# Weight tiles of the FFN: two buffers for weight sums and six for plain blocks become one ring of eight fixed tiles

## Chip, cores and metric

The kernel runs on one core of one Trainium2 chip. The metric is the device time of one execution in microseconds (us). A measurement of this kernel can tell about 0.2%, some 4.2 us, from no change.

## What is computed

The reference is a decoder trunk of two layers over a residual stream of 256 tokens by 2048 columns, all float32:

```python
for layer in range(DEPTH):                       # DEPTH = 2
    xn = rms_norm(h, norm_mix[layer])
    mix = swa_mlstm_mixer(xn, ...) if layer % 2 == 0 else forgetting_attention_mixer(xn, ...)
    h = h + mix                                  # both end in ... @ w_out
    h = h + swiglu(rms_norm(h, norm_ffn[layer]), w_gate[layer], w_up[layer], w_down[layer])
return rms_norm(h, norm_final)

def swiglu(xn, w_gate, w_up, w_down):            # 2048 -> 5632 -> 2048
    return (jax.nn.silu(xn @ w_gate) * (xn @ w_up)) @ w_down
```

Layer 0 mixes with sliding-window attention and an mLSTM side by side, layer 1 with a forgetting attention of 16 heads. Each mixer ends in an output projection (2048 by 2048), and the FFN follows.

## The kernel before, in words

**Split products.** [...] A weight block arrives by DMA as `raw` (128 x 1024, two k-tiles of 512 columns); ScalarE copies it to `hi` (line 180), VectorE forms `lo = raw - hi` (line 181), and TensorE adds three products per k-tile and half of the tokens: hi by hi, lo by hi, hi by lo (`three`, line 524, and lines 215 to 217 in `gemm`). So each weight byte costs a cast on ScalarE and a subtraction on VectorE before TensorE may read it.

**Chunks and blocks.** `gemm` (line 196) runs a projection as a row of such chunks. The FFN and some other products run in `pair_group` (line 532): two matrices side by side, walked in blocks of two k-tiles. A plain block (kind 0) takes one chunk of each matrix: two `hi`/`lo` pairs, 24 matmuls. A mixed block (kind 1) replaces products of the two token halves and the two matrices by sums, in the manner of Strassen: 21 matmuls instead of 24, but VectorE forms four sums of weights (lines 601 to 604), and four pairs are split: the first matrix's chunk (`hg`, `lg`), half a chunk of the second (`hu`, `lu`, line 600), and two pairs of sums, called the halves (`hs`, `ls`, line 613; their tiles are `ht` and `lt`).

**Buffers.** `hi` and `lo` come from the pool `wp`, six buffers each (line 103). The halves come from the FFN's own pool `fp`, two buffers each of `ht` and `lt` (lines 611 and 612), that is, just one mixed block's worth. Outside the FFN, mixed blocks use other spare memory for their halves (`spare_halves`, line 494). `raw` has four buffers in `wr` for plain chunks and four in `fp` for mixed blocks. The pool `fp` opens in `close_layer` (line 759), which runs the output projection (`out_proj`, line 503) and then the FFN (`ffn`, line 632); its memory is what the mixers' pools have given back.

**Order.** The FFN is cut into parts of 3, 4 and 4 column groups (`PARTS`), each followed by its share of the down projection. A group walks eight blocks in `ORDER` (five plain, three mixed) or, for the groups in `DENSE` (1, 4, 6, 8), in `HEAVY` (four and four); `DOWN` does the same for the down projection. Transposes of the activations run by DMA and are joined some blocks later (`join`, line 695). The Tile framework orders each engine's instructions when the kernel is built, and every engine then works through its own fixed order, waiting on semaphores. The loads of weights are all issued by SyncE, in the order in which the program names them. The output projection's chunks are ordered among the last steps of the mixer (the mLSTM heads, `mlstm`, line 1073, in layer 0; the last quarter of the attention, `attention`, line 372, in layer 1): its products over the first twelve k-tiles need nothing of those steps.

Of the kernel before, what the change touches and what calls it, by code (L numbers as in the profile page):

```python
# [9 lines left out]
F32R = mybir.dt.float32r  # L10
# [7 lines left out]
P = 128  # L18
# [5 lines left out]
NB = 512  # L24
CK = 2
# [50 lines left out]
def trunk(  # L76
# [23 lines left out]
    xl = sp_.tile([P, KT, S], F32R, name="xl")  # L100
    mh = sp_.tile([P, KT, S], F32R, name="mh")
    ml = sp_.tile([P, KT, S], F32R, name="ml")
    wp = ctx.enter_context(tc.tile_pool(name="wp", bufs=6))
    wr = ctx.enter_context(tc.tile_pool(name="wr", bufs=4))
    cp = ctx.enter_context(tc.tile_pool(name="cp", bufs=1))
    sm = ctx.enter_context(tc.tile_pool(name="sm", bufs=2))
# [65 lines left out]
    def load_chunk(w, k0, c0, n):  # L172
        raw = ahead.pop(0) if ahead else load_raw(w, k0, c0, n)
        return raw if isinstance(raw, tuple) else split_chunk(raw, n)

    def split_chunk(raw, n):
        hi = wp.tile([P, CK, NB], F32R, tag="hi", name="hi")
        lo = wp.tile([P, CK, NB], F32R, tag="lo", name="lo")
        for k in (slice(0, 1), slice(1, CK)) if any(raw is f for f in fine) else (slice(0, CK),):
            latest[0] = nc.scalar.copy(hi[:, k, 0:n], raw[:, k, 0:n])  # L180
            nc.vector.tensor_tensor(  # L181
                out=lo[:, k, 0:n], in0=raw[:, k, 0:n], in1=hi[:, k, 0:n].bitcast(F32), op=ALU.subtract
            )
        return hi, lo
# [6 lines left out]
    def run_due(todo, step):  # L191
        while todo and todo[0][0] <= step:
            with tc.issue_after(latest[0].ins):
                todo.pop(0)[1]()
# [334 lines left out]
    def bank(par, name):  # L529
        return pm.tile([P, NB], F32, tag="pm", name=name) if par else pa.tile([P, NB], F32, tag="acc", name=name)  # L530

    def pair_group(fp, par, lhs, sums, mats, order, todo=(), halves=None, inner=None, raws=None):
        plain = [[bank(par, "acc") for _ in range(NT)] for _ in range(2)]
        begun = set()

        def fresh(*at):
            known = at in begun
            begun.add(at)
            return not known

        todo = list(todo)
        prods = None
        kinds = [kind for kind, _ in order]
        t0, t1 = slice(0, P), slice(P, 2 * P)

        def combine(prods):
            c = fp.tile([P, 4, NB], F32, tag="c", name="c", bufs=1)
            nc.scalar.copy(c[:, 0, :], prods[0])
            if halves is None:
                nc.vector.tensor_tensor(out=c[:, 1, :], in0=prods[3], in1=c[:, 0, :], op=ALU.add)  # L550
                nc.vector.tensor_tensor(out=c[:, 2, :], in0=prods[2], in1=c[:, 1, :], op=ALU.add)  # L551
                nc.vector.tensor_tensor(
                    out=c[:, 1:4:2, :],
                    in0=prods[1].rearrange("p (a n) -> p a n", a=1).broadcast_to([P, 2, NB]),
                    in1=c[:, 1:3, :],
                    op=ALU.add,
                )
                return c
            nc.vector.tensor_tensor(out=c[:, 2, :], in0=prods[3], in1=c[:, 0, :], op=ALU.add)
            nc.vector.tensor_tensor(out=c[:, 1, :], in0=prods[2], in1=c[:, 2, :], op=ALU.add)  # L560
            nc.vector.tensor_tensor(out=c[:, 3, :], in0=prods[1], in1=c[:, 1, :], op=ALU.add)
            nc.vector.tensor_tensor(out=c[:, 2, :], in0=prods[1], in1=c[:, 2, :], op=ALU.add)
            return c

        for pos, (kind, pair) in enumerate(order):
            k0 = 2 * pair
            if inner is not None and pos == len(order) - 1:
                c = combine(prods)
                inner()
            if not kind:  # L570
                last = pos == len(order) - 1
                walk = [(i, t) for i in range(CK) for t in range(NT)]
                if last:
                    walk.sort(key=lambda it: it[1])
                for m, (w, c0) in enumerate(mats):
                    hi, lo = load_chunk(w, k0, c0, NB)
                    run_due(todo, pos)
                    for i, t in walk:
                        ah, al = lhs(k0 + i)
                        ts = slice(t * P, (t + 1) * P)  # L580
                        three(
                            plain[m][t], ah[:, ts], al[:, ts], hi[:, i, :], lo[:, i, :],
                            fresh(m, t), last and i == CK - 1,
                        )
                continue
            first, last = 1 not in kinds[:pos], 1 not in kinds[pos + 1 :]
            if first:
                prods = [bank(1 - par, "prod") for _ in range(4)]
            ra, rb = (load_raw(w, k0, c0, NB, fp, W_RAWS if halves else RAWS, raws) for w, c0 in mats)
            hg, lg = split_chunk(ra, NB)  # L590
            run_due(todo, pos)
            t4 = ra if halves else fp.tile([P, 2, NB], F32, tag="t4", name="t4", bufs=1)
            ta, tb, tc_, td = (
                (ra[:, 0, :], rb[:, 0, :], rb[:, 1, :], ra[:, 1, :])
                if halves
                else (t4[:, 0, :], t4[:, 1, :], ra[:, 0, :], ra[:, 1, :])
            )
            hu = wp.tile([P, CK, NB], F32R, tag="hi", name="hi")
            lu = wp.tile([P, CK, NB], F32R, tag="lo", name="lo")
            split_plain(hu[:, 1, :], lu[:, 1, :], rb[:, 1, :])  # L600
            nc.vector.tensor_tensor(out=ta, in0=rb[:, 0, :], in1=ra[:, 0, :], op=ALU.subtract)
            nc.vector.tensor_tensor(out=tb, in0=rb[:, 1, :], in1=rb[:, 0, :], op=ALU.subtract)
            nc.vector.tensor_tensor(out=tc_, in0=rb[:, 1, :], in1=ta, op=ALU.subtract)
            nc.vector.tensor_tensor(out=td, in0=ra[:, 1, :], in1=tc_, op=ALU.subtract)
            parts = []
            for src in (ra, rb) if halves else (t4, ra):
                if halves:
                    hs, ls = halves.pop(0)
                    halves.append((hs, ls))
                else:  # L610
                    hs = fp.tile([P, 2, NB], F32R, tag="ht", name="ht")
                    ls = fp.tile([P, 2, NB], F32R, tag="lt", name="lt")
                split_plain(hs, ls, src)
                parts.append((hs, ls))
            where = ((0, 0), (1, 0), (1, 1), (0, 1)) if halves else ((0, 0), (0, 1), (1, 0), (1, 1))
            ht = [parts[a][0][:, b, :] for a, b in where]
            lt = [parts[a][1][:, b, :] for a, b in where]
            sh, sl = sums(pair)
            xa, la = lhs(k0)
            xb, lb = lhs(k0 + 1)  # L620
            three(prods[0], xa[:, t0], la[:, t0], hg[:, 0, :], lg[:, 0, :], first, last)
            three(plain[0][0], xb[:, t0], lb[:, t0], hg[:, 1, :], lg[:, 1, :], fresh(0, 0), False)
            three(plain[1][0], sh[3], sl[3], hu[:, 1, :], lu[:, 1, :], fresh(1, 0), False)
            three(prods[1], sh[0], sl[0], ht[0], lt[0], first, last)
            three(prods[2], sh[2], sl[2], ht[1], lt[1], first, last)
            three(prods[3], sh[1], sl[1], ht[2], lt[2], first, last)
            three(plain[0][1], xb[:, t1], lb[:, t1], ht[3], lt[3], fresh(0, 1), False)
        if inner is None:
            c = combine(prods)
        return plain, c  # L630
# [128 lines left out]
    def close_layer(layer, w_out, idx, key, **rest):  # L759
        with tc.tile_pool(name=f"fp{layer}", bufs=2) as fp:  # L760
            nx = len(mixed_of(ORDER))
            nd = max(len(mixed_of(o)) for o in DOWN.values())
            sx = [fp.tile([P, nx, 4, P], F32R, name=f"sx{i}", bufs=1) for i in range(2)]
            x4 = fp.tile([P, 2, P], F32R, name="x4", bufs=1)
            todo = out_proj(w_out, idx, key, (*sx, x4, fp))
            sd = [fp.tile([P, nd, 4, P], F32R, tag=f"sd{i}", name=f"sd{i}", bufs=1) for i in range(2)]
            ffn(layer, fp, sx, x4, sd, key, todo, **rest)


    acc0 = new_acc()  # L770
    hi = wp.tile([P, CK, NB], F32R, tag="hi", name="hi")
    lo = wp.tile([P, CK, NB], F32R, tag="lo", name="lo")
    latest[0] = latest_warm
    for k in range(CK):
        with tc.issue_after(latest[0].ins):
# [594 lines left out]
```

## Time and profile before

| | |
|---|---|
| median of 3 runs | 2111.59 us (2111.06 to 2115.66) |
| the profiled execution | 2111.82 us |
| its span in the profile | 2110.1 us |
| mean granted TensorE clock | 0.997 |
| VectorE busy | 1854.7 us, 88% |
| ScalarE busy | 1387.9 us, 66% |
| moved by DMA | 434.87 MB, 206 GB/s on average |

Engines: PE is TensorE's matmuls, PEld its weight loads, DVE VectorE, ACT ScalarE, POOL GpSimd, SP SyncE. A group's row gives line, engine, operation and tiles, the count, busy time, mean time of one in ns, and the idle time before them with what ended it. A row of the timeline gives start and duration in us; the bracket is the idle time before it and what ended it. A row of stretches gives each engine's busy time in that stretch and, in brackets with an x, how many instructions it began. Matmuls overlap in the pipeline, so the pace of PE is read from one start to the next.

### The profile page before, as it was taken

The numbers are of one execution on the slowest core, as the hardware profiler recorded it, in microseconds if no ns is written. First come the engines' busy times: TensorE is split into PE (matmuls) and PEld (weight loads), VectorE is DVE, ScalarE is ACT, GpSimd is POOL, SyncE is SP. The second block draws the span as 40 slices with busy tenths as digits, with TensorE's granted clock in tenths as the row PEclk, the third lists the DMA queues.
The fourth block names the chain that finished last, engine by engine and source line by source line (L and its number), as shares of the span: only waits on it lengthen the run. The fifth ranks groups of instructions, "written<-read, shape, count | busy, mean of one in ns | idle before, by whom it ended". The sixth has DMA issues, their size and how long they took to land.

```text
span 2110.1 us, 26965 instructions
## 1 busy us (share of the span) xinstructions
PE 2073.6 (98%) x9449; PEld 1710.7 (81%) x9449; DVE 1854.7 (88%) x2415; ACT 1387.9 (66%) x1760; POOL 43.2 (2%) x66
## 2 busy tenths in 40 slices
PE   9999999999999999999999999999999999999998
PEld 7878888778887788888888888888778887788887
DVE  6788769999998999999899678689999999999995
ACT  6767678665576656666667676687655666556763
POOL 1010100000000000000000001000000000000000
PEclk9999999999999999999999999999999999999999
DMA  8666677666666666766667766596656666756664
GB/s 289 176 201 200 202 238 215 198 209 196 190 217 204 216 195 206 229 201 202 199 196 215 221 201 184 155 276 202 223 188 204 209 203 187 236 191 211 217 189 153
DMA packets 309575, 434.87 MB, mean 206 GB/s; under 512 B 106412, under 2 KB 114624, under 8 KB 309312
## 3 DMA queue, kind: packets, MB, share of 16 engines
q1 hardware_dynamic: 307088, 426.27, 65.4%
q0 software_dynamic: 1632, 5.80, 0.9%
q8 instruction: 74, 1.21, 0.2%
q10 hardware_dynamic: 720, 1.09, 0.1%
q14 instruction: 61, 0.50, 0.1%
HBM read 408.68 MB, written 2.12 MB: 195 GB/s over the span
## 4 chain that ended last, share of the span: by engine, by line
PE 85%; DVE 7%; DMA 3%; issue 2%; ACT 2%; SPq 0%; POOLq 0%; POOL 0%; DVEq 0%; ACTq 0%
PE acc L525 18%; PE acc L526 17%; PE acc L527 17%; PE acc L216 5%; PE acc L215 5%; PE acc L217 5%; PE prod L525 5%; PE prod L527 4%; PE prod L526 4%; DVE lo L181 2%; DMA raw<-in_w_down_dram 2%; DVE lt L350 1%; DMA raw<-in_w_up_dram 1%; PE p L379 1%; PE po L480 1%
## 5 line engine op out<-in xcount | busy, mean ns | idle before, releaser
L180 ACT CAST hi<-raw 128x1024 fp32r<-128x1024 f32 (+3 forms) x648 | 655.2, 1027 | 372.4 <-PE acc L527 216.3
L181 DVE TENSOR_TENSOR lo<-raw,hi 128x1024 fp32r<-128x1024 f32 (+3 forms) x648 | 761.8, 1190 | 115.7 <-ACT hi L180 112.5
L526 PE MATMUL acc<-lo,xh 128*128 128x512 f32 x1198 | 467.2, 390 | 0.0
L527 PE MATMUL acc<-hi,xl 128*128 128x512 f32 x1198 | 463.8, 390 | 0.0
L525 PE MATMUL acc<-hi,xh 128*128 128x512 f32 x1198 | 461.2, 391 | 0.1
L525 PEld LDWEIGHTS acc<-hi,xh 128*128 128x128 f32 x1198 | 225.1, 188 | 48.3 <-DVE c L551 0.8
L526 PEld LDWEIGHTS acc<-lo,xh 128*128 128x128 f32 x1198 | 225.2, 188 | 47.3 <-DVE lo L181 0.8
L527 PEld LDWEIGHTS acc<-hi,xl 128*128 128x128 f32 x1198 | 225.2, 188 | 47.0
L349 ACT CAST ht<-t 128x1024 fp32r<-128x1024 f32 x103 | 108.4, 1052 | 113.6 <-PE prod L527 80.5
L525 PE MATMUL acc<-hi,mh 128*128 128x512 f32 x437 | 167.0, 393 | 10.0 <-ACT mh L349 5.0
L526 PE MATMUL acc<-lo,mh 128*128 128x512 f32 x437 | 170.4, 390 | 0.0
L527 PE MATMUL acc<-hi,ml 128*128 128x512 f32 x437 | 166.1, 389 | 0.0
L350 DVE TENSOR_TENSOR lt<-t,ht 128x1024 fp32r<-128x1024 f32 x103 | 125.6, 1219 | 23.5 <-ACT ht L349 22.7
L350 DVE TENSOR_TENSOR lt<-raw,ht 128x1024 fp32r<-128x1024 f32 x103 | 125.3, 1217 | 3.2 <-ACT ht L349 3.0
L216 PE MATMUL acc<-lo,mh 128*128 128x512 f32 (+1 forms) x322 | 126.3, 392 | 0.0
L215 PE MATMUL acc<-hi,mh 128*128 128x512 f32 (+1 forms) x322 | 125.8, 391 | 0.0
L217 PE MATMUL acc<-hi,ml 128*128 128x512 f32 (+1 forms) x322 | 123.7, 391 | 0.0
L349 ACT CAST hi<-raw 128x512 fp32r<-128x512 f32 x117 | 72.4, 619 | 71.4 <-PE acc L527 49.9
L349 ACT CAST ht<-raw 128x1024 fp32r<-128x1024 f32 x103 | 108.0, 1049 | 13.7 <-PE acc L527 10.2
L525 PEld LDWEIGHTS acc<-hi,mh 128*128 128x128 f32 x437 | 82.0, 188 | 31.6 <-ACT mh L349 6.4
L216 PE MATMUL acc<-lo,xh 128*128 128x512 f32 (+3 forms) x288 | 100.1, 348 | 0.2 <-DVE lo L181 0.2
L217 PE MATMUL acc<-hi,xl 128*128 128x512 f32 (+3 forms) x288 | 99.4, 346 | 0.0
(382 smaller groups left out, 3575.8 us busy)
## 6 DMA issues: line engine op xcount, KB each, us to landing
raw<-in_w_gate_dram SPq DMA_DIRECT2D x176, 512.0 KB, 4.4
raw<-in_w_up_dram SPq DMA_DIRECT2D x176, 512.0 KB, 4.5
raw<-in_w_down_dram SPq DMA_DIRECT2D x176, 512.0 KB, 4.8
raw<-in_w_in_odd_dram SPq DMA_DIRECT2D x88, 512.0 KB, 4.9
raw<-in_w_in_even_dram SPq DMA_DIRECT2D x51, 512.0 KB, 5.0
raw<-in_w_out_even_dram SPq DMA_DIRECT2D x32, 512.0 KB, 5.1
raw<-in_w_out_odd_dram SPq DMA_DIRECT2D x32, 512.0 KB, 4.8
hr<-in_w_in_even_dram SPq DMA_DIRECT2D x12, 512.0 KB, 4.5
```

The source lines that it names most:

```text
L180: latest[0] = nc.scalar.copy(hi[:, k, 0:n], raw[:, k, 0:n])
L181: nc.vector.tensor_tensor(out=lo[:, k, 0:n], in0=raw[:, k, 0:n], in1=hi[:, k, 0:n].bitcast(F32), op=ALU.subtract)
L215: nc.tensor.matmul(o, ah[:, ts], hi, start=(k == 0), stop=False)
L216: nc.tensor.matmul(o, ah[:, ts], lo, start=False, stop=False)
L217: nc.tensor.matmul(o, al[:, ts], hi, start=False, stop=(k == k_all - 1 and cs.stop == n))
L349: nc.scalar.copy(dst_h, src)
L350: nc.vector.tensor_tensor(out=dst_l, in0=src, in1=dst_h.bitcast(F32), op=ALU.subtract)
L379: nc.tensor.matmul(pq[j % 2][:, j // 2, :], q_of(j, b), k_of(j)[:, 0:cols], start=True, stop=True)
L480: nc.tensor.matmul(po, v_of(j, 0), tt[:, j, 0:2, :].rearrange("p c q -> p (c q)"), start=True, stop=False)
L525: nc.tensor.matmul(o, ah, hi, start=start, stop=False)
L526: nc.tensor.matmul(o, ah, lo, start=False, stop=False)
L527: nc.tensor.matmul(o, al, hi, start=False, stop=stop)
```

## The change

The pool `wp` keeps six pairs of tiles, now with fixed names, in a list; `slot()` takes the oldest pair and puts it at the list's end. `close_layer` makes two further pairs in `fp`, in the place of the two buffers each of `ht` and `lt`, and appends them to the list before the output projection; at the end of the layer they leave it. Everything that is split in the FFN, plain chunks and halves alike, and also the chunks of the output projection, takes its pair from this ring of eight. The bytes in use are the same: two buffers each of `ht` and `lt` before, two pairs `hi6`, `lo6`, `hi7`, `lo7` after.

```diff
-    wp = ctx.enter_context(tc.tile_pool(name="wp", bufs=6))
+    wp = ctx.enter_context(tc.tile_pool(name="wp", bufs=1))
+    weights = [[wp.tile([P, CK, NB], F32R, name=f"{a}{i}") for a in ("hi", "lo")] for i in range(6)]
+
+    def slot():
+        weights.append(weights.pop(0))
+        return weights[-1]
...
     def split_chunk(raw, n):
-        hi = wp.tile([P, CK, NB], F32R, tag="hi", name="hi")
-        lo = wp.tile([P, CK, NB], F32R, tag="lo", name="lo")
+        hi, lo = slot()
...
-            hu = wp.tile([P, CK, NB], F32R, tag="hi", name="hi")
-            lu = wp.tile([P, CK, NB], F32R, tag="lo", name="lo")
+            hu, lu = slot()
...
                 else:
-                    hs = fp.tile([P, 2, NB], F32R, tag="ht", name="ht")
-                    ls = fp.tile([P, 2, NB], F32R, tag="lt", name="lt")
+                    hs, ls = slot()
                 split_plain(hs, ls, src)
...
             x4 = fp.tile([P, 2, P], F32R, name="x4", bufs=1)
+            more = [[fp.tile([P, CK, NB], F32R, name=f"{a}{i}", bufs=1) for a in ("hi", "lo")] for i in (6, 7)]
+            weights.extend(more)
             todo = out_proj(w_out, idx, key, (*sx, x4, fp))
             sd = [fp.tile([P, nd, 4, P], F32R, tag=f"sd{i}", name=f"sd{i}", bufs=1) for i in range(2)]
             ffn(layer, fp, sx, x4, sd, key, todo, **rest)
+            for pair in more:
+                weights.remove(pair)
```

The very first chunk of the kernel takes its pair by `slot()` too.

More of the change, by code (lines that the diff above doesn't have):

```diff
@@ L767, in close_layer @@
             ffn(layer, fp, sx, x4, sd, key, todo, **rest)
+            for pair in more:
+                weights.remove(pair)
     acc0 = new_acc()
-    hi = wp.tile([P, CK, NB], F32R, tag="hi", name="hi")
-    lo = wp.tile([P, CK, NB], F32R, tag="lo", name="lo")
+    hi, lo = slot()
     latest[0] = latest_warm
```

## The prediction, made before the changed kernel was run

> **What bounds the kernel now.** I read the page's busy times first:
>
> ```profile
> span 2110.1 us, 26965 instructions
> PE 2073.6 (98%) x9449; PEld 1710.7 (81%) x9449; DVE 1854.7 (88%) x2415; ACT 1387.9 (66%) x1760; POOL 43.2 (2%) x66
> ```
>
> PE has 36.5 us of idle time in all; only what returns some of it, or lets matmuls run closer together, can help. So next I cut the span into stretches of 50 us and looked for those in which PE is not full. A full one stands first, then the eight in the two FFNs that are not:
>
> ```profile
> core 0: us, PE busy (x) PEld busy (x) DVE busy (x) ACT busy (x) POOL busy (x), PEclk, DMA share, GB/s
> 500.00:550.00 50.00, 50.00 (x223) 41.40 (x222) 47.30 (x54) 27.72 (x31) 0.00 (x0) 1.00 0.66 211
> 400.00:450.00 50.00, 47.11 (x198) 37.68 (x197) 45.68 (x58) 31.47 (x35) 0.00 (x0) 0.97 0.66 205
> 450.00:500.00 50.00, 47.16 (x208) 37.88 (x207) 47.91 (x59) 26.14 (x30) 0.00 (x0) 1.00 0.59 187
> 650.00:700.00 50.00, 45.61 (x193) 35.32 (x192) 44.57 (x56) 30.79 (x35) 0.00 (x0) 1.00 0.61 190
> 700.00:750.00 50.00, 48.21 (x210) 38.99 (x209) 48.29 (x56) 31.58 (x33) 0.00 (x0) 1.00 0.67 204
> 1450.00:1500.00 50.00, 48.23 (x210) 38.79 (x209) 46.26 (x59) 32.64 (x37) 0.00 (x0) 1.00 0.65 200
> 1500.00:1550.00 50.00, 47.87 (x212) 38.48 (x211) 48.32 (x60) 33.38 (x38) 0.00 (x0) 1.00 0.68 216
> 1700.00:1750.00 50.00, 48.92 (x214) 39.61 (x212) 42.97 (x57) 33.91 (x37) 0.00 (x0) 1.00 0.68 200
> 1750.00:1800.00 50.00, 44.84 (x188) 34.61 (x189) 49.22 (x59) 34.14 (x38) 0.00 (x0) 1.00 0.67 209
> ```
>
> Two readings. PE is idle for 22.1 us in these eight (50 less each PE busy time, added). But they begin 1633 matmuls where eight full stretches would begin 8 x 222 = 1776: 143 are missing, and at 50 / 222 = 0.225 us each that is **32 us lost**, 10 more than the idle time. VectorE is at 86 to 98% in the same rows, so it has hardly any reserve when it falls behind. The timeline of PE at the first stop shows where the other 10 us are:
>
> ```profile
> 401.06 0.61 PE L525 MATMUL prod<-ht,xh 128*128 128x512 f32 x2
> 404.13 0.50 PE L525 MATMUL prod<-ht,xh 128*128 128x512 f32 x1 [2.45 <-ACT ht L349]
> ...
> 406.66 0.63 PE L526 MATMUL acc<-lo,xh 128*128 128x512 f32 x1
> 407.08 0.63 PE L527 MATMUL acc<-hi,xl 128*128 128x512 f32 x1
> ...
> 408.61 0.40 PE L525 MATMUL acc<-hi,xh 128*128 128x512 f32 x1
> ```
>
> After a stop of 2.45 us the matmuls start 0.42 us apart instead of 0.225 for a while. From 401.06 to 408.61 PE begins 14 matmuls; at full pace they take 3.2 us, here 7.55: the stop with its tail costs 4.4 us, 1.9 more than its length. PE waited for a half (`ht`). What PE waits for in all, and what holds the halves up, is told by the lists of waits of PE and ScalarE, and by VectorE's timeline in the costliest stretch:
>
> ```profile
> PE prod L526 <- DVE lt L350: 5.1, 5, 1.6
> PE prod L525 <- ACT ht L349: 4.4, 4, 2.5
> PE pt L282 <- DVE h L363: 3.7, 1, 3.7
> ACT ht L349 <- PE prod L527: 80.5, 48, 4.1
> 670.24 1.23 DVE L350 TENSOR_TENSOR lt<-t,ht 128x1024 fp32r<-128x1024 f32 x1 [3.27 <-ACT ht L349]
> ```
>
> The halves stand at the head of PE's waits (5.1 and 4.4 us). 48 times a cast into `ht` waits until PE has read the half before it, and at 670 VectorE stands idle for 3.27 us behind such a cast, in a stretch where it is the engine that is late.
>
> **Part 1, the FFN: what the ring gives.** No instruction is added or removed; the built program has the same count on every engine. What moves is which matmul frees the buffer of a cast, and with it the order. In the built orders I counted the matmuls between the last reader of a buffer and the first reader of its next content: for a half the median rises from 28 to about 50, for a plain chunk it falls slightly, from 46 to 44; the tightest twentieth is 16 to 18 in both. So halves gain 5 us of room (22 x 0.225) and plain chunks give up 0.5. The half that was cast just before 670 is freed, in the new assignment, by a matmul that runs at 648 in the trace of before: 20 us earlier.
>
> What that is worth I add up along the queues. A stop arises where, from the matmul that frees a buffer, the queued work of ScalarE and VectorE up to a later operand of PE lasts longer than PE's own matmuls in between. The prices:
>
> ```profile
> L180 ACT CAST hi<-raw 128x1024 fp32r<-128x1024 f32 (+3 forms) x648 | 655.2, 1027 | 372.4 <-PE acc L527 216.3
> L350 DVE TENSOR_TENSOR lt<-t,ht 128x1024 fp32r<-128x1024 f32 x103 | 125.6, 1219 | 23.5 <-ACT ht L349 22.7
> 664.36 0.68 DVE L601 TENSOR_TENSOR t<-raw 128x512 f32<-128x512 f32 x1
> 664.96 0.68 DVE L602 TENSOR_TENSOR t<-raw 128x512 f32<-128x512 f32 x1
> raw<-in_w_down_dram SPq DMA_DIRECT2D x176, 512.0 KB, 4.8
> ```
>
> In a full queue a large VectorE operation takes 1.14 us (a little under its 1.22, since they overlap) and a small one 0.60 (664.96 - 664.36). From the cast before 670 to the matmul that needs the transposed activations (`mh`) stand that cast and a copy (2.8 us), 19 large and 24 small VectorE operations and four tiny ones (37.2 us), one load that they hold back (4.7 us), and three casts and two copies behind it (5.7 us): 50.4 us, against 193 matmuls, 43.8 us. PE comes 6.6 us short. The same walk gives 6.1 us for the stops from 400 to 460, and 6.2 and 6.6 us for their twins in layer 1: 25.6 us in all, between the 22.1 us of idle time and the 32 us with the slow matmuls, which is how far I trust it. Along the built order of the changed kernel, at the same prices, 0.6, 1.4 and 1.4 us remain in layer 0 and 1.4 and 1.4 in layer 1: 6.3 us. Three quarters go: **32 x 19.3 / 25.6 = 24 us gained**. The bounds: no gain, if VectorE is late anyway; 32 us, if every stop goes. The next thing that is late is VectorE itself, in the dense groups.
>
> **Part 2, the output projections: what the ring costs.** The two further pairs join the ring before the output projection, and they lie in `fp`, over memory that the mixer still uses: in layer 0 over the output gates and mLSTM matrices, in layer 1 over the queries, keys and transposed probabilities of the last quarter. Chunks 7 and 8 of each output projection fall to these pairs, and cannot be cast before the mixer has ended. This is an added wait. Behind it stand: the two `raw` tiles that hold these chunks, half of the four that plain loads have; and on PE the chunks' matmuls, which the built order puts behind the mixer's last steps. In before those matmuls are the cover of these steps:
>
> ```profile
> 257.30 0.87 DVE L1097 SCALAR_TENSOR_TENSOR hv<-hv,st,og 128x256 f32<-128x256 f32 x2
> 261.14 0.27 PE L1124 MATMUL ptv<-ident,hv 128*128 128x128 f32 x1
> 1334.15 1.92 DVE L426 TENSOR_SCALAR s<-s,rec 128x128 f32<-128x128 f32 x8
> 1338.86 0.27 PE L466 MATMUL pp<-ident,s 128*128 128x128 f32 x1
> ```
>
> In layer 1 the scaled probabilities are ready at 1336.1 and PE takes them at 1338.9: 2.8 us of reserve. In the changed order 57 matmuls (12.9 us) that stood between the scores and this transpose stand behind it, none ahead. 12.9 - 2.8 = 10.1 us are uncovered; the copy after the transposes, so far behind 15 further matmuls that also move, adds about 0.4, and late loads (below) some. I take 11.5. In layer 0 the head's result is ready at 258.2 and taken at 261.1, a reserve of 3.0 us; 56 matmuls (12.7 us) move behind. That would uncover 9.7 us, but here part of the moved matmuls stood ahead of the mLSTM's own matmuls too, so the chain starts earlier; its queues added up give 6.7. I take 7. The bounds: 5.4 us at each place if only the two chunks' own 24 matmuls count, less the reserve, so 5 in all; and 25.6 if no reserve helps. Each stop is followed by slow matmuls, 1.9 us by the row at 404: 3.8. **Loss 11.5 + 7 + 3.8 = 22 us.**
>
> [...]
>
> **Part 3, the rest.** The two pairs that hold `ht` and `lt` are replaced byte for byte, the six old pairs turn as before, and the mixers' own blocks keep their halves elsewhere. Their order shifts a little, and PE is full there, as the stretches around the two output projections show:
>
> ```profile
> 250.00:300.00 50.00, 50.00 (x226) 41.30 (x226) 30.47 (x49) 35.48 (x59) 1.38 (x2) 1.00 0.65 197
> 1300.00:1350.00 50.00, 50.00 (x249) 42.32 (x248) 33.92 (x49) 27.46 (x42) 1.03 (x1) 1.00 0.62 190
> ```
>
> I price the shift at nothing, from -2 to +2 us. The stop between the layers, 3.7 us before `pt` in the list of waits above, does not hang on weight buffers and stays.
>
> **The sum.** 2111.8 (the profiled execution) - 24 + 22 = **2110 us**, 0.1% below it and below the median of 2111.59, which lies 0.2 us under that execution.
>
> **Rivals.**
> *The stops at the output projections are cheap.* If the scheduler's shift lets the attention and mLSTM chains run as much earlier as PE is freed, only the two chunks' own matmuls lack, less the reserves: 2 x 5.4 - 2.8 - 3.0 = 5 us, with slow tails about 9. Then 2111.8 - 24 + 9 = 2097 us. For it: VectorE does fewer subtractions between scores and probabilities in the new order. Against it: the scores themselves don't come earlier in layer 1.
> *The locked loads decide (slower).* With two of four `raw` tiles held, the next six chunks load in pairs, each pair after the one before it:
>
> ```profile
> raw<-in_w_out_even_dram SPq DMA_DIRECT2D x32, 512.0 KB, 5.1
> raw<-in_w_out_odd_dram SPq DMA_DIRECT2D x32, 512.0 KB, 4.8
> ```
>
> A round is 4.8 to 5.1 + 1.03 + 1.22 = 7.1 to 7.3 us for 24 matmuls, 5.4 us. If PE has nothing else, three rounds cost 3 x 1.7 = 5 us in each layer, 10 in all: 2120 us. It decides from the point at which PE has used what was cast before chunk 7; in the trace those chunks run beside other matmuls, which speaks for less.
> *Short stops do not slow PE.* If the slow matmuls belong to something other than the stops, the FFN can give back only idle time, 22.1 x 3/4 = 17 us, while the two long stops still have their tails: 2111.8 - 17 + 22 = 2117 us. [...]
>
> **How the numbers follow.** The forecast, gain and loss nearly cancelling (2104 to 2116): 0.40. Cheap stops, 2097: 0.26. Locked loads, 2120: 0.26. Short stops free, 2117: 0.08. Of the forecast's 0.40 I put 0.10 on faster by over 0.2% (below 2107.4), 0.24 within 0.2%, which is about what a measurement can tell, and 0.06 slower (above 2115.8). So faster 0.36, same 0.24, slower 0.40. The range takes in the centres of both sides, 2096 to 2122: the bounds of parts 1 and 2 reach further (2085 to 2137), but only with every term at its end.
>
> **What would show it.** Right: in the FFNs' stretches PE begins 215 to 222 matmuls everywhere and the waits for `ht` and `lt` shrink from 9.5 us to under 4. Near 250 and 1320 PE has stops of 6 to 12 us, ended by the mixer's last steps (`ptv`, `pp`), with ScalarE's casts of chunks 7 and 8 after them. Loads of the output projection land in pairs 7 us apart. Wrong: PE full at 250 and 1320 (part 2 falls), or FFN stretches still at 190 to 210 (part 1 falls, VectorE being the bound).

## The result, and the profile after

The changed kernel takes 2116.76 us (median of 10 runs, 2115.35 to 2118.14) against 2111.97 us of the kernel before: a ratio of 1.0021, 95% interval [1.0011, 1.0031]. (One of the ten runs of the kernel before took 2599.66 us; the ratio leaves it out.) It is 4.8 us slower where 2 us faster was forecast; that is just about what a measurement can tell. The profiled execution took 2116.89 us, with this span and PE row:

```profile
span 2115.2 us, 26817 instructions
PE 2074.0 (98%) x9449; PEld 1714.0 (81%) x9449; DVE 1851.3 (88%) x2415; ACT 1382.6 (65%) x1760; POOL 40.8 (2%) x66
```

The totals say nothing: PE's busy time differs by 0.4 us, and each engine has as many instructions as before (the total, 26817 for 26965, counts waiting and issuing instructions too). The stretches of 50 us do. These are the FFNs' eight, with the same columns as in the prediction; the matmuls that ran in a stretch, the one or two under way at its start included, stand behind PE's busy time:

```profile
400.00:450.00 50.00, 48.14 (x212) 39.22 (x211) 48.83 (x64) 35.75 (x41) 0.00 (x0) 1.00 0.70 227
450.00:500.00 50.00, 49.41 (x219) 39.83 (x218) 47.93 (x58) 27.65 (x32) 0.00 (x0) 1.00 0.64 215
650.00:700.00 50.00, 48.23 (x212) 39.14 (x211) 49.21 (x62) 33.10 (x37) 0.00 (x0) 1.00 0.68 216
700.00:750.00 50.00, 50.00 (x223) 41.39 (x222) 47.67 (x57) 30.90 (x34) 0.00 (x0) 1.00 0.62 202
1450.00:1500.00 50.00, 47.89 (x204) 39.14 (x203) 47.24 (x61) 33.34 (x37) 0.00 (x0) 0.97 0.67 205
1500.00:1550.00 50.00, 50.00 (x221) 41.20 (x220) 49.64 (x63) 32.68 (x37) 0.00 (x0) 1.00 0.63 211
1700.00:1750.00 50.00, 49.46 (x218) 40.63 (x217) 46.99 (x60) 35.76 (x39) 0.00 (x0) 1.00 0.59 180
1750.00:1800.00 50.00, 48.75 (x215) 39.92 (x214) 50.00 (x62) 35.92 (x39) 0.00 (x0) 1.00 0.67 214
```

Against 222 matmuls in a full stretch, 22 are missing in layer 0 (the first four rows) and 30 in layer 1. Before, it was 79 and 64. So 57 came back in layer 0 and 34 in layer 1: 91 x 0.225 = 20.5 us. The stretches around the two output projections, full before, went the other way:

```profile
250.00:300.00 50.00, 45.18 (x191) 36.61 (x192) 27.32 (x38) 32.20 (x50) 1.38 (x2) 0.91 0.59 161
1300.00:1350.00 50.00, 39.08 (x190) 32.41 (x189) 30.20 (x46) 24.96 (x41) 0.63 (x1) 0.90 0.46 137
```

They hold 191 matmuls instead of 226 and 190 instead of 249. The list of PE's waits names the stops (total us, times, longest us):

```profile
PE pp L471 <- DVE s L431: 10.5, 1, 10.5
PE acc L220 <- ACT mh L359: 6.9, 1, 6.9
PE acc L530 <- ACT c L553: 3.8, 2, 2.1
PE prod L530 <- DVE xl L360: 3.1, 1, 3.1
PE acc L531 <- DVE lo L186: 2.9, 4, 1.2
...
PE prod L530 <- ACT hi L354: 1.1, 2, 0.5
```

The waits for `ht` and `lt` that led the list before are gone (the halves are now called `hi` and `lo`). At the head stand two stops that the kernel before did not have: 10.5 us before the transposes of the probabilities (layer 1) and 6.9 us before the output projection's own matmuls, which need `mh`, the mixer's activations (layer 0). The stop of 3.7 us before `pt`, which the prediction left in its place, is gone; the one of 3.1 us behind `xl` (the low part of the activations, formed on VectorE) is new.

For a ledger I compared the start of a PE instruction in two traces wherever both programs have sent PE the same instructions up to it (within a few that changed places at the ends of a layer). The difference of two such points says what the stretch between them cost or gave, in us against the trace of before:

| stretch of the span before | forecast | changed | changed, 2nd trace | E1 | E1, 2nd trace | E3 |
|---|---|---|---|---|---|---|
| 184 to 276: output projection, layer 0 | +8.9 | +12.4 | +12.9 | +2.3 | +1.9 | +1.8 |
| 300 to 735: FFN, layer 0 | -12 | -12.3 | -12.5 | -10.6 | -11.2 | -5.1 |
| 735 to 1303: rest of layer 0, mixer of layer 1 | 0 | +1.0 | +1.4 | +2.5 | +2.1 | +4.8 |
| 1303 to 1354: output projection, layer 1 | +13.4 | +12.7 | +12.9 | +0.2 | +0.1 | +0.2 |
| 1369 to 1810: FFN, layer 1 | -12 | -8.0 | -9.4 | -8.8 | -7.7 | 0.0 |

E1 and E3 are experiments below. In the changed kernel the two projections lose 25.1 us and the FFNs give back 20.3.

### The profile page after: what moved, and what is told of

Its sections match the earlier page's. It is cut to its first block, busy times and chain, and to the rows that moved or that the text cites. A ratio compares the mean times of both kernels' runs of the same rounds, so it can differ in the third digit from the quotient of the medians.

```text
span 2115.2 us, 26817 instructions
## 1 busy us (share of the span) xinstructions
PE 2074.0 (98%) x9449; PEld 1714.0 (81%) x9449; DVE 1851.3 (88%) x2415; ACT 1382.6 (65%) x1760; POOL 40.8 (2%) x66
## 4 chain that ended last, share of the span: by engine, by line
PE 82%; DVE 7%; DMA 4%; ACT 3%; issue 3%; SPq 0%; ACTq 0%; POOLq 0%; POOL 0%; DVEq 0%
PE acc L531 18%; PE acc L532 17%; PE acc L530 17%; PE acc L221 5%; PE acc L220 5%; PE acc L222 5%; PE prod L530 4%; PE prod L532 4%; PE prod L531 4%; DVE lo L186 3%; DVE lo L355 2%; ACT hi L185 1%; DMA raw<-in_w_up_dram 1%; DMA raw<-in_w_down_dram 1%; DMA raw<-in_w_in_odd_dram 1%
## 5 line engine op out<-in xcount | busy, mean ns | idle before, releaser
L531 PE MATMUL acc<-lo,xh 128*128 128x512 f32 x1272 | 495.4, 390 | 0.2 <-DVE lo L186 0.2
L532 PE MATMUL acc<-hi,xl 128*128 128x512 f32 x1272 | 493.4, 390 | 0.0
L530 PE MATMUL acc<-hi,xh 128*128 128x512 f32 x1272 | 479.4, 391 | 3.8 <-ACT c L553 3.8
L532 PEld LDWEIGHTS acc<-hi,xl 128*128 128x128 f32 x1272 | 239.3, 188 | 49.8
L354 ACT CAST hi<-raw 128x512 fp32r<-128x512 f32 (+1 forms) x220 | 179.3, 819 | 72.2 <-PE acc L532 44.6
L355 DVE TENSOR_TENSOR lo<-raw,hi 128x512 fp32r<-128x512 f32 (+1 forms) x220 | 204.8, 933 | 11.9 <-ACT hi L354 11.9
L354 ACT CAST hi<-t 128x1024 fp32r<-128x1024 f32 x103 | 108.3, 1051 | 85.3 <-PE prod L532 65.5
L355 DVE TENSOR_TENSOR lo<-t,hi 128x1024 fp32r<-128x1024 f32 x103 | 125.4, 1217 | 11.0 <-ACT hi L354 10.7
L531 PEld LDWEIGHTS acc<-lo,mh 128*128 128x128 f32 x466 | 87.5, 188 | 21.9 <-DVE lo L186 3.9
L532 PEld LDWEIGHTS acc<-hi,ml 128*128 128x128 f32 x466 | 87.5, 188 | 18.1
```

Of the source, the lines that this page charges most:

```text
L354: nc.scalar.copy(dst_h, src)
L355: nc.vector.tensor_tensor(out=dst_l, in0=src, in1=dst_h.bitcast(F32), op=ALU.subtract)
L530: nc.tensor.matmul(o, ah, hi, start=start, stop=False)
L531: nc.tensor.matmul(o, ah, lo, start=False, stop=False)
L532: nc.tensor.matmul(o, al, hi, start=False, stop=stop)
```

## The experiments

The theory after the result: loss and gain are two things with different causes. The loss comes from one chunk in the output projection that cannot be cast before the mixer has ended, and from everything on PE that stands behind it; the gain comes from the later reuse of the halves' buffers, and the stops that remain in the FFN are VectorE's own lateness. The rivals are named with each run.

### Loss and gain taken apart: E1, E2 and E3

E1 lets the two pairs join the ring only behind the output projection:

```
             more = [[fp.tile([P, CK, NB], F32R, name=f"{a}{i}", bufs=1) for a in ("hi", "lo")] for i in (6, 7)]
-            weights.extend(more)
             todo = out_proj(w_out, idx, key, (*sx, x4, fp))
+            weights.extend(more)
```

> The two further pairs join the ring only after the output projection, so that its 32 chunks turn over the six old pairs and the FFN alone over eight. Theory (the two effects are separate: the output projections lose 12.4 and 13.5 us because chunks 7 and 8 fall to pairs over the mixer's memory; the FFNs gain 12.2 and 8.3 us through the ring of eight): the stops of 6.9 and 10.5 us before acc and pp are gone, the FFNs' gain stays, and the time is 2112.0 - 12.2 - 8.3 = 2091.5 us (2087 to 2094). Rival 1 (the stops come from the fixed tiles or from the shifted order of the whole program, not from where the pairs lie): the stops stay, 2110 to 2117 us. Rival 2 (the FFN's gain is only ScalarE and VectorE catching up after a late output projection): without the late start the gain goes too, 2106 to 2112 us.

E2 gives the ring of eight to the output projections alone:

```
             todo = out_proj(w_out, idx, key, (*sx, x4, fp))
+            for pair in more:
+                weights.remove(pair)
+            own[:] = more
...
-                    hs, ls = slot()
+                    own.append(own.pop(0))
+                    hs, ls = own[-1]
```

> The ring of eight serves the output projections alone; for the FFN the two further pairs leave it and hold the halves of the weight sums, as ht and lt did before. Theory (losses and gains are separate and add): 2112.0 + 12.4 + 13.5 = 2137.9 us (2134 to 2141), with the stops before acc (layer 0) and pp (layer 1) at 6 to 11 us. Rival (a late output projection is made up in the FFN whatever its buffers are): 2118 to 2128 us.

E3 has the fixed tiles and shares nothing: `weights.extend(more)` is replaced by `own[:] = more`, ahead of the output projection, and the halves turn over `own` as in E2.

> Only the form is changed: the six pairs are fixed tiles that turn by hand, and the halves turn over two fixed pairs of their own; nothing is shared. Theory: the buffers free as in the kernel before, 2112 us, within 2 us. Rival (fixed tiles make the scheduler order the work in another way and carry part of the loss): 2115 us or more.

| kernel | ring of eight in the projection | in the FFN | median us | ratio to before, 95% interval |
|---|---|---|---|---|
| E3 | no | no | 2114.03 | 1.0002 [0.9993, 1.0012] |
| E2 | yes | no | 2138.71 | 1.0122 [1.0105, 1.0139] |
| E1 | no | yes | 2095.92 | 0.9917 [0.9902, 0.9931] |
| changed | yes | yes | 2116.76 | 1.0021 [1.0011, 1.0031] |

The fixed tiles by themselves change nothing that can be measured. Joining before the projection costs 24.7 us (E2 - E3) or 20.8 (changed - E1); joining for the FFN gives 18.1 us (E3 - E1) or 22.0 (E2 - changed). The changed kernel's row was measured at another time: the kernel before took 2111.97 us beside it and 2113.66 us beside the other three, so the two differences that use it are uncertain by some 2 us. E2 met its number (2137.9). E1 took 2095.92 us where 2091.5 was expected, above its range of 2087 to 2094. By the ledger its FFNs give 19.4 us, about 2 us of the loss in layer 0 stays, and 2.5 us go between the two. The same 2 us in layer 0 stand in E3, so they belong to the shifted order that the fixed tiles bring and not to the locked pairs. (E3's FFN gains 5.1 us in layer 0 up to 735 and gives 4.8 back by 1303, some 3.3 of them between 960 and 1036, around the FFN's own end; why was not tried.) In E1's list of waits the two long stops are gone, and nothing over 3.1 us is left:

```profile
PE acc L531 <- DVE lo L186: 5.0, 6, 1.4
PE prod L530 <- DVE xl L360: 3.1, 1, 3.1
PE prod L530 <- ACT hi L354: 1.8, 4, 0.5
```

That joining for the FFN gives the 18 us is shown by E1 and E3. That it does so through the halves' buffers is argued from PE's list, where the waits for halves shrink. ScalarE's own waits are no measure of it: its casts of the first pair of sums into a half wait 80.5 us for PE in the kernel before, 56.7 in E3, which shares nothing and gains nothing, and 58.6 in E1. Most of these waits never reach PE, which before waits 9.5 us in all for `ht` and `lt`.

E1 is the version that beats both kernels. It and the changed kernel were measured once more, without any edit, to see how far the shares repeat:

> The kernel with the pairs joining after the output projection once more: 2096 us, to see whether the FFNs' gains by layer (10.5 and 8.6 us in its first trace) repeat within 1 us.

> The changed kernel once more, beside the others on the same chip: 2116.8 us. Its trace says how far the shares of the two layers (12.4 and 13.5 us lost, 12.2 and 8.3 us gained) repeat; if they are properties of the program, each comes back within 1 us, and if they scatter from run to run, by 2 to 3 us.

They came to 2095.33 us, 0.9913 [0.9898, 0.9928], and 2116.84 us, 1.0014 [1.0004, 1.0023]. In the ledger each share comes back within 1.4 us; layer 1's FFN is the one that misses the 1 us, by 0.4 in the changed kernel and 0.1 in E1. Still it gives 7.7 to 9.4 us in all four traces and layer 0's 10.6 to 12.5, so the difference between the layers is larger than the scatter.

### What the locked chunk costs, and how: E4, E7 and E6

E4 lets one pair join before the projection and the other behind it:

```
-            weights.extend(more)
+            weights.append(more[0])
             todo = out_proj(w_out, idx, key, (*sx, x4, fp))
+            weights.append(more[1])
```

> Only one of the two pairs joins before the output projection, so chunk 7 alone of each falls to memory that the mixer still uses and three raw tiles stay free; the other pair joins after it, and the FFN has eight. In the built order the matmuls between the scores of layer 1 and the transposes of the probabilities are 4, as with two pairs (59 where none joins), since chunk 7 is the first of the second accumulators and the chunks behind it cannot pass it. Theory (the loss is set by how many matmuls stand behind the first locked chunk, not by the number of locked pairs or raw tiles): the stops before pp and acc stay at 7 to 10 us and 6 to 7 us, and the time is within 4 us of the changed kernel's, 2113 to 2118 us. Rival (the loss goes by the locked pairs: half of them, half of it): 2096 + 11 = 2107 us, stops of 3 to 5 us.

E7 also locks one pair, but a count in `slot()` puts it into the ring when the projection's chunk 12 is due:

```
     def slot():
+        if count[0] == 0 and late:
+            weights.insert(0, late.pop())
+        count[0] -= 1
...
-            weights.extend(more)
+            count[0] = 11
+            late[:] = more[:1]
             todo = out_proj(w_out, idx, key, (*sx, x4, fp))
+            weights.append(more[1])
```

> One pair joins before the output projection again, but in such a way that chunk 12 of each falls to it, and not chunk 7; the other pair joins after it. In the built order 59 matmuls stay between the scores and the transposes of layer 1, and 12 matmuls move behind the values' products. Theory (what counts is what stands behind the first locked chunk): 12 matmuls are 2.7 us, the stops of 7 and 10 us are gone, and the time is 2096 to 2100 us. Rival (a locked pair costs the same wherever it falls in the projection): as with the pair at chunk 7.

E4: 2118.60 us, 1.0023 [1.0013, 1.0032], 0.6 us above its range; beside it the changed kernel took 2116.84 us, so one locked pair costs as much as two. E7: 2098.73 us, 0.9926 [0.9912, 0.9941]; the same one pair, five chunks later, costs 3 us, and not in the projections: by the ledger they lose 1.9 and 0.1 us, as in E1, while the FFNs give 8.9 and 5.4 instead of 10.6 and 8.8. Its time is in the expected range, but the 2.7 us that were expected for the 12 moved matmuls are not where they were expected; why the FFNs give less was not tried. In E4's list both stops stand:

```profile
PE pp L471 <- DVE s L431: 7.5, 1, 7.5
PE acc L220 <- ACT mh L359: 7.1, 1, 7.1
```

Of the two places tried, what sets the price is that of the first locked chunk. The built orders say why: between the last scores of layer 1 and the first transpose of the probabilities stand 66 of the projection's matmuls in the kernel before, 59 in E1 and E7, but 4 in the changed kernel and in E4. Chunk 7 is the first of the second accumulators; chunks 8 to 12 add to the same accumulators and come after it in the built order, locked or not.

E6 asks how much of the rest are late loads: chunks 9 to 14 are cast from the raw tile of chunk 6.

```
+        at[0] += 1
+        if 9 <= at[0] <= 14:
+            raw = sixth[0]
+        else:
+            raw = ahead.pop(0) if ahead else load_raw(w, k0, c0, n)
```

> As the changed kernel, but chunks 9 to 14 of each output projection are not loaded: they are cast from the raw tile of chunk 6 (that part of the projection is left out, since other weights are multiplied). So no load can be late behind the two raw tiles that chunks 7 and 8 hold, while the same casts and matmuls remain. Theory A (the matmuls that moved behind the mixer's last steps lack as cover, which is how the forecast's 11.5 and 7 us were made): the stops before pp (10.5 us) and acc (6.9 us) stay within 2 us of that. Theory B (the loads that come late, in pairs 6 us apart, hold the casts, and these hold the softmax's steps on VectorE): the stop of layer 1 falls below 4 us and the layer loses under 5 us; layer 0's stop falls as well if it has the same cause, and stays if it is the transposition of the head's result alone. Time by A 2113 to 2117 us, by B 2100 to 2108 us.

2115.75 us, 1.0008 [0.9997, 1.0018], and the stops stay, somewhat shorter:

```profile
PE acc L227 <- ACT mh L366: 7.1, 2, 6.4
PE pp L478 <- DVE s L438: 7.0, 1, 7.0
```

In layer 0 that is within theory A's 2 us (6.4 for 6.9). In layer 1 the stop shrinks by 3.5 us to 7.0, which meets neither theory: most of it is the lost cover, and a part is late loads. In the changed kernel the loads can be seen on ScalarE, with the start, the length, and in brackets the idle time ahead:

```profile
1319.93 1.05 ACT L185 CAST hi<-raw 128x1024 fp32r<-128x1024 f32 x1 [1.60 <-DMA raw<-in_w_out_odd_dram]
1323.32 1.05 ACT L185 CAST hi<-raw 128x1024 fp32r<-128x1024 f32 x1 [2.34 <-DMA raw<-in_w_out_odd_dram]
1325.98 1.05 ACT L185 CAST hi<-raw 128x1024 fp32r<-128x1024 f32 x1 [1.61 <-DMA raw<-in_w_out_odd_dram]
1329.40 1.04 ACT L185 CAST hi<-raw 128x1024 fp32r<-128x1024 f32 x1 [2.38 <-DMA raw<-in_w_out_odd_dram]
```

A pair of casts every 6.07 us (1319.93 to 1325.98, 1323.32 to 1329.40): the rounds that the rival "locked loads" described, at 6.07 us for its 7.1 to 7.3. They reach the path through VectorE: in the trace the mask of the scores (1328.20) comes behind a subtraction (1327.06) that had waited 1.43 us for such a cast:

```profile
1327.06 1.23 DVE L186 TENSOR_TENSOR lo<-raw,hi 128x1024 fp32r<-128x1024 f32 x1 [1.43 <-ACT hi L185]
1328.20 0.75 DVE L387 SCALAR_TENSOR_TENSOR s<-p,cb 128x256 f32<-128x256 f32 x2
```

By the ledger's way of counting, layer 1's projection loses 12.7 us with two raw tiles held, 10.9 in E4 with one, and 9.8 in E6 without the loads. So 2 to 3 us are the loads and 10 the lost cover. In layer 0 the three lose 12.4, 12.0 and 11.3 us.

### What is left in the FFN: E8 and E9

E8 is E1 without two of the four subtractions that make the weight sums in the FFN:

```
-            nc.vector.tensor_tensor(out=tc_, in0=rb[:, 1, :], in1=ta, op=ALU.subtract)
-            nc.vector.tensor_tensor(out=td, in0=ra[:, 1, :], in1=tc_, op=ALU.subtract)
+            if halves:
+                nc.vector.tensor_tensor(out=tc_, in0=rb[:, 1, :], in1=ta, op=ALU.subtract)
+                nc.vector.tensor_tensor(out=td, in0=ra[:, 1, :], in1=tc_, op=ALU.subtract)
```

> The pairs join after the output projection (2096 us), and in the FFN two of the four subtractions that make the weight sums are left out (the sums are then not those of the reference): VectorE has 2 x 0.60 us less to do for each mixed block, and every buffer stays as it was. It asks what holds the 13 us of stops that the ring of eight leaves in the FFNs. Theory (VectorE comes late in the dense groups): the waits for lo and hi shrink, the FFN's windows at 202 to 215 matmuls rise to 218 to 222, and the time falls by 6 to 12 us to 2084 to 2090. Rival (the remaining stops are again waits for buffers, or ScalarE's casts): less than 3 us, 2093 to 2097.

2074.72 us, 0.9812 [0.9798, 0.9827]: 21 us below E1, nearly twice the upper end of what was expected. Buffers and ScalarE's work are untouched, and PE is full in these FFN stretches:

```profile
400.00:450.00 50.00, 50.00 (x222) 41.46 (x221) 46.78 (x57) 34.08 (x37) 0.00 (x0) 1.00 0.73 225
650.00:700.00 50.00, 50.00 (x222) 41.43 (x222) 43.95 (x52) 37.55 (x41) 0.00 (x0) 1.00 0.72 222
1450.00:1500.00 50.00, 50.00 (x222) 41.46 (x221) 46.71 (x56) 34.94 (x39) 0.00 (x0) 1.00 0.72 233
1750.00:1800.00 50.00, 50.00 (x222) 41.44 (x221) 42.73 (x45) 27.72 (x30) 0.00 (x0) 1.00 0.71 227
```

So the stops that the ring leaves are VectorE's lateness. Whether it is VectorE's load as a whole, or the row of four subtractions that must end before the sums can be cast, E8 doesn't tell: both shrink in it. The surplus over the forecast lies mostly elsewhere: 6.5 us came at 988 to 1003 us of E1's trace, in the layer's last down projection, where the 3.1 us wait for `xl` and the slow matmuls behind it went too.

E9 asks whether that relief can be had without leaving work out. It is E1 with one of the four subtractions, the one that writes `tb`, on GpSimd in the FFN (`nc.gpsimd.tensor_tensor` for `nc.vector.tensor_tensor`).

> The pairs join after the output projection (2096 us), and one of the four subtractions of each mixed block of the FFN, 103 in all, goes to the idle GpSimd; nothing is left out. The trace with two of them left out showed 2074.7 us, so VectorE's work is what remains late. Theory (VectorE's load decides, and GpSimd works beside it): half of that relief, 103 x 0.60 us, gives about half the gain, 2083 to 2090 us. Rival (GpSimd's subtraction is long, or the two hinder each other, so that the sums' casts come later than now): 2096 us or more.

2111.66 us, 0.9987 [0.9977, 0.9996]: 16 us worse than E1, as the rival had it. Two rows of E9 by engine and shape (total us, mean ns) show the price:

```profile
L606 POOL TENSOR_TENSOR t<-raw 128x512 f32<-128x512 f32 x103 | 354.9, 3446 | 1094.4 <-DVE lo L355 726.6 <-DVE raw L607 134.1 <-DMA raw<-in_w_up_dram 73.8
...
L605 DVE TENSOR_TENSOR t<-raw 128x512 f32<-128x512 f32 x103 | 94.4, 917 | 6.6 <-DMA raw<-in_w_up_dram 4.7 <-DMA raw<-in_w_down_dram 1.8
```

and the same two lines in E1:

```profile
L605 DVE TENSOR_TENSOR t<-raw 128x512 f32<-128x512 f32 x103 | 70.7, 686 | 6.7 <-DMA raw<-in_w_up_dram 5.4 <-DVE ml L355 0.6 <-DMA raw<-in_w_down_dram 0.3
L606 DVE TENSOR_TENSOR t<-raw 128x512 f32<-128x512 f32 x103 | 70.6, 686 | 0.0
```

The subtraction takes 3.45 us on GpSimd instead of 0.69, and the one that stands ahead of it on VectorE 0.92 instead of 0.69. Nor is VectorE relieved: it is busy for 1858.7 us in E9, with 103 subtractions fewer, against 1851.6 us in E1. And the sums come later: ScalarE's casts wait 74.9 us in all for GpSimd's `t`. How much of the 16 us is each was not tried.

## Why the prediction was wrong, point by point

The two mechanisms, buffers that free earlier in the FFN and lost cover at the projections, were right; the terms nearly cancelled, and their errors decided the sign. Of the signs named ahead, the waits for halves and the stop at `pp` came as said; three FFN stretches stayed at 204 to 212 matmuls, below 215, and the stop in layer 0 was not at `ptv` (point 3). From -2 to +5.1 us in the trace are 7 us, and four terms make them up.

1. **"32 x 19.3 / 25.6 = 24 us gained" (part 1) is the step that failed most: 20.3.** All of it lies in layer 1, which gave 8.0 to 9.4 where an even split gives 12; layer 0 gave its 12. Two things were wrong. The walk along the queues gave the stops of layer 1 the same length as "their twins" in layer 0, but the stretches quoted beside it held 79 missing matmuls in layer 0 and only 64 in layer 1. The twin of the stop at 404 shows why, in the trace of before:

```profile
1481.62 0.50 PE L525 MATMUL prod<-ht,xh 128*128 128x512 f32 x1 [1.63 <-ACT ht L349]
1481.96 0.40 PE L525 MATMUL acc<-ht,xh 128*128 128x512 f32 x1
```

   It is 1.63 us long, not 2.45, and no slow matmuls follow it. And more stops were left in layer 1 than the walk left: 30 matmuls are missing, 6.8 us, where 2.8 of the 6.3 us were put there. Among them is the one of 2.1 us before `acc` behind ScalarE's `c`.
2. **"I price the shift at nothing" (part 3): +2 in layer 0.** The matmuls between the mLSTM's last product and the transposes of its result (`ptv`) are 37 before and 23 in E1, which has no locked chunk. E1 and E3 lose 1.8 to 2.3 us there. But PE doesn't stop before `ptv` in E1. It stops at two weight chunks of the projection near 263 and 266, for 0.9 and 0.6 us, as two further rows of E1's list of waits show:

```profile
PE acc L220 <- ACT hi L185: 0.9, 1, 0.9
PE acc L221 <- DVE lo L186: 0.8, 2, 0.6
```

   So the loss comes with the new order; that the 14 matmuls of cover cause it is not shown. The bound of 2 was just about reached; the value taken was too small.
3. **"I take 7" plus a tail of 1.9 (part 2, layer 0): 10.4**, that is 12.4 less the 2 of point 2. The stop was 6.9 us long, as forecast, but it is another stop: the forecast's 7 us were worked out for the transposes on PE (`ptv`) of a late head, and PE doesn't stop there. It stops ahead of them (`ptv` starts at 259.67) before matmuls that need `mh` of an earlier head, which is transposed by DMA. ScalarE waits for that DMA and then makes `mh`:

```profile
252.67 1.38 ACT L338 COPY room<-hv 128x512 uint16<-128x512 uint16 x2 [3.02 <-DMA hv<-room]
254.08 0.91 ACT L359 ACTIVATE mh<-room,gT 128x256 fp32r<-128x256 f32 x2
```

   So the kind of cause was right, cover that moved away from a step of the mixer, but the step was wrong, and that the length agrees is luck. The tail was longer than the 1.9:

```profile
254.64 0.80 PE L220 MATMUL acc<-hi,mh 128*128 128x512 f32 x1 [6.93 <-ACT mh L359]
255.24 0.63 PE L221 MATMUL acc<-lo,mh 128*128 128x512 f32 x1
255.66 0.63 PE L220 MATMUL acc<-hi,mh 128*128 128x512 f32 x1
```

   The starts stay 0.42 us apart for ten matmuls, which is 2.2 us, and another 0.8 went at 265 to 269. In layer 1 "I take 11.5" with its tail was 12.7 for 13.4, at the stop that was forecast. But its parts were not: the forecast left about 1 us for late loads where E6 and E4 show 2 to 3, and so 12.4 for the lost cover where 10 remain; it counted 57 moved matmuls where the built orders have 66 - 4 = 62. The two places together, 23.1 for 22, agree to 5% partly by luck. What E4 and E7 do show is that the matmuls behind the locked chunk, and not the number of locked pairs, are the measure.
4. The remaining 0.3 us lies at the start, at the end and in the stretch from 735 to 1303.

The rivals: "the stops at the output projections are cheap" (2097) falls with the two stops. "The locked loads decide" (2120) had the right mechanism in a small part, 2 to 3 us in layer 1 and at most 1.1 in layer 0; its time is near the result for another reason. "Short stops do not slow PE" is half right, as the last section shows. The bounds of parts 1 and 2 held, that of part 3 was just about reached, and the range held the time; only the sum stood on the wrong side of zero.

What told the parts apart in advance was at hand: with two terms of 20 us and opposite sign, the useful finding was not the sum but that they have different places in the program. E1 follows from the prediction's part 2 alone.

## What to carry to other kernels

When buffers join a rotation, ask for each of its users when their memory is free, and let them join behind the last user that would have to wait: the same two pairs cost 21 to 25 us from before the projection and nothing from behind it. One buffer that comes late costs what stands behind its chunk in the accumulation and in the engine's order; the number of such buffers hardly mattered here (one pair at chunk 7: as much as two; at chunk 12: nothing in the projections). A sum of two large terms with opposite sign has the errors of both: count each from the stretch where it arises, layer by layer, and don't carry one layer's stop over to its twin.

## What the runs showed of the hardware that was not expected

**How long PE may stand before its matmuls slow down.** Two stops of the changed kernel of the same kind, at 414 and at 1494 us:

```profile
414.40 0.50 PE L530 MATMUL acc<-hi,xh 128*128 128x512 f32 x1 [1.68 <-ACT c L553]
414.74 0.39 PE L531 MATMUL acc<-lo,xh 128*128 128x512 f32 x1
414.97 0.40 PE L532 MATMUL acc<-hi,xl 128*128 128x512 f32 x1
```

```profile
1494.62 0.52 PE L530 MATMUL acc<-hi,xh 128*128 128x512 f32 x1 [2.11 <-ACT c L553]
1494.96 0.61 PE L531 MATMUL acc<-lo,xh 128*128 128x512 f32 x1
1495.37 0.63 PE L532 MATMUL acc<-hi,xl 128*128 128x512 f32 x1
```

Behind 1.68 us the next starts are 0.23 us apart, behind 2.11 us they are 0.41 to 0.43 apart for eight matmuls, which makes this stop cost 4.0 us (11 starts from 1492.12, the last before it, to 1498.61: 6.49 us, where full pace takes 2.5). Over all traces here, of 32 stops of 1.2 to 2.0 us ahead of 512-wide matmuls two were followed by a run of slow ones; of 18 from 2.1 to 7.1 us, 17 were (5 to 13 matmuls). In the traces of before and of the changed kernel alone, none of the eight of 1.23 to 1.68 us was, and all four of 2.11, 2.45, 3.12 and 6.93 us were. So the prediction's tail is right for the long stops and wrong for most of the FFN's, which are shorter.

That also corrects where "the other 10 us" of the eight FFN stretches went. By the starts in the trace of before, the matmuls that start 0.42 us apart cost 1.7 us there, nearly all behind the stop at 404. Most of the rest, some 9 us, is spread over 24 short stops, about 0.4 us each: a stop costs more than its idle time, because idle time is counted from the end of a matmul of 0.39 us, where the next could have started after 0.227, and because the first starts behind a stop are further apart, as the 0.34 us behind 414.40 show. So short stops give back more than their idle time too: in the eight stretches PE's idle time fell by 13.9 us, from 22.1 to 8.1, and 20.5 us came back.

**GpSimd as a helper for VectorE.** A float32 subtraction of 128x512 took 3.45 us there against 0.69 on VectorE, and VectorE's own subtraction just ahead of it in the program grew by a third, from 686 to 917 ns, in the same kernel. What made it grow was not shown: no run here separates GpSimd's work beside it from other causes.
